# PE's order in the mixer stretches of a two-layer hybrid decoder trunk fixed to the order in which the program emits it

## The chip, the cores and the metric

The kernel runs on one core of one Trainium2 chip. The metric is the device time of one execution in microseconds (us). A core has five engines that run their own instruction streams and wait for one another on semaphores: PE (TensorE, matrix products), DVE (VectorE), ACT (ScalarE), POOL (GpSimd) and SP (SyncE, which here only issues DMAs). PEld in the profile is PE's weight load, which overlaps its matmuls.

## The reference

One step of a trunk with two layers: 256 tokens of a new prompt, and 8 samples of 8 tokens each with 2,048 cached tokens behind them. The kernel keeps both together as T = 320 columns.

```python
def trunk(...):
    for l in range(DEPTH):                     # 2 layers, D_MODEL 1024, D_FF 2816
        x = x + 0.5 * swiglu(rms_norm(x, W['norm_ffn1'][l]), W['ffn1_wi'][l], W['ffn1_wo'][l])
        p = rms_norm(x, W['norm_mix'][l]) @ W['w_in'][l]
        p_hg, p_rw, p_mla = jnp.split(p, [HG_COLS, HG_COLS + RW_COLS], axis=-1)
        o_hg, hg_s = hgrn2_mixer(p_hg, lbs[l], W['hg_norm'][l], hg_s0[l])       # 4 heads of 64
        o_rw, rw_s, rw_sh = rwkv7_mixer(p_rw, rw_sh0[l], rw_s0[l], l, W)        # 4 heads of 64
        q_nope, q_pe, c, k_pe = mla_project(p_mla, pos, l, W)
        o_mla = attend(l, q_nope, q_pe, c, k_pe)      # 8 heads; samples read pages of a cache
        o = jnp.concatenate([o_hg, o_rw, o_mla], axis=-1)
        x = x + o @ W['w_out'][l]
        x = x + 0.5 * swiglu(rms_norm(x, W['norm_ffn2'][l]), W['ffn2_wi'][l], W['ffn2_wo'][l])
    y = rms_norm(x, W['norm_final'])
```

Everything is float32. The outputs are y and the new recurrent states and cache rows.

## The kernel before

x lies transposed, with features on the partitions and the 320 tokens in the columns. Each dense product (the feed-forward parts, the in-projections, w_out) is done with 128x128 weight blocks that are split into a high and a low part in fp32r, by an ACT cast (`split`, L422) and a DVE subtraction (L423); three matmuls of 320 columns make one block (`dense_steps`, `dense_pair`). The weights of the feed-forward parts are streamed on SP's queue, those of the mixers on ACT's, 512 columns at a time.

The program is: first feed-forward part, mixer of layer 0, second and first feed-forward parts, mixer of layer 1, last feed-forward part. In the profiled execution the two mixer stretches lie at about 223 to 613 us and 1051 to 1445 us. A mixer (`mixer`, L550) computes:

- `mla_in` and `mla_q`, the in-projections of the attention, in a plain sequence;
- then two weaves. The first has `rw` (RWKV-7, for each pair of heads `hp` a preparation, a triangular inverse by levels, then `seq` and chunks of 64 tokens), `rw_out`, `sample` (attention over the cached pages: scores into `S`, `exps` at L890, transposes of `S` into `pa` banks, sums with the pages into `pv`) and a `fill` of dense in-projections (`rw_in`, `hg_in`). The second weave has `hg` (HGRN2), `prompt` (the prompt's attention, in `heads`), the rest of `sample`, and `w_out`.

The small sums of `rw` and `hg` are in plain fp32 on 64 partitions each: two heads lie in the two halves of the partitions, `R2 = [slice(0, 64), slice(64, 128)]`, and a loop `for r in R2` emits the matmul of each half. The sums of `sample` have 64 weight columns (96x64 or 128x64). Products into one PSUM bank go by the tags `pd` (2 banks), `pr` (3), `pa` (2) and `pv` (1).

**What sets PE's order.** `weave` (L513) steps the generators. It keeps a planned clock of PE, `self.pe`, which `mm` (L286) and `tr` (L290, transposes) advance; each `yield` names a delay or a due time after which its stream may go on, and the weave takes the first stream that is due. The streams of `rw`, `hg` and `prompt` are urgent: their delays are stretched by `LAG = 2.8`, and what they emit gets a higher priority:

```python
with self.tc.high_priority(offset=1000) if g in self.urgent else ExitStack():
    r = next(g)
f = LAG if g in self.urgent else 1
```

The order that comes out is not the order in which PE runs. The scheduler behind the program (`TileContext(nc, schedule_with_timeline_sim=True)`) takes, on each engine, the ready instruction of the highest priority by its own estimate of the time. So in the mixers a matmul of an urgent stream stands in the middle of another stream's sum as soon as it is thought to be ready, and a dense product is cut into pieces.

The places that the prediction speaks of: the end of `rw_in` and the preparation in `rw` (L1009 to L1056: sigmoid, tanh, sqrt and exp on ACT, a scan, two reciprocals L1039 and products on DVE); `scores`, `soft` and `exps` of `sample` (L871 to L890) with the transposes that follow; `heads` (softmax on DVE L782 to L800 and ACT L796); the ten products into `EX` and `ES` in `hg` (exp at L1330); `mla_in`. In the changed kernel these lines lie 8 to 23 lines further down, `mm` at L294 and `tr` at L298.

Of the kernel before, what the change touches and what calls it, by code (L numbers as in the profile page):

```python
# [19 lines left out]
T = 320  # L20
# [25 lines left out]
FINAL = [(0, 1), (1, 1), (2, 2), (4, 2), (6, 1), (7, 1)]  # L46
FPOOL = (1, 4)
R2 = [slice(0, 64), slice(64, 128)]


KR = 96
# [205 lines left out]
class Kern:  # L257
    def __init__(self, ctx, tc, ap):
        self.ctx, self.tc, self.nc, self.ap = ctx, tc, tc.nc, ap
        P = lambda name, bufs, **k: ctx.enter_context(tc.tile_pool(name=name, bufs=bufs, **k))  # L260
        self.cp = P("cp", 1)
        self.xp = P("xp", 1)
        self.wp = P("wp", 1)
        self.ps = P("ps", 1, space=bass.MemoryType.PSUM)
        self.n = 0
        self.gat, self.early, self.casts = [], [], []
        self.pe = 0.0

        self.st = {"wf": [FBLK, 0, None, None], "wm": [MBLK, 0, self.wp, None]}
        self.cur = "wf"  # L270
# [9 lines left out]
        return self.t(self.ps, [128, 512], tag, bufs=self.BANKS[tag])  # L280


    def mm(self, out, w, x, start, stop):
        m, n = (int(np.prod(a.shape[1:])) for a in (w, x))
        c = max(n, 2 * m) if w.dtype == F32R else 4 * max(n, m)
        self.last = self.nc.tensor.matmul(out, w, x, start=start, stop=stop)  # L286
        self.pe += max(c / 2400 * (0.58 if m <= 64 else 1), 0.032)

    def tr(self, out, x, ident):
        self.nc.tensor.transpose(out, x, ident)  # L290
        self.pe += 0.11 if x.shape[0] > 64 else 0.05

    def tr2(self, out, x, idt):
# [254 lines left out]
            yield from g  # L548

    def mixer(self, l):  # L550
        nc, tc = self.nc, self.tc
        self.l = l
        self.pe, self.ready, self.ended, self.ev = 0.0, {}, [], {}
        xh, xl = self.tiles(self.xh, KD), self.tiles(self.xl, KD)
        pool = lambda name: tc.tile_pool(name=f"{name}{l}", bufs=1)
        with pool("mx") as self.mp, pool("ms") as self.sp, tc.tile_pool(name=f"mk{l}", bufs=1, side="right") as self.tb:
            self.idx_setup(l)
            with pool("mq") as self.ta:
                self.mla_in(xh, xl)
                self.mla_q()  # L560
            sample = self.sample()
            with pool("mr") as self.ta:
                rin = self.rw_in(xh, xl)
                for _ in range(17):
                    next(rin)
                rw = [self.together(*[self.chain(self.rw(hp), self.rw_out(hp)) for hp in range(2)])]
                fill, rws = self.chain(rin, self.hg_in(xh, xl), self.outs()), self.rw_split()
                self.urgent = [*rw, rws]
                self.weave([*rw, *ORDER_A(fill, sample), rws], [*rw, fill, rws])
            with pool("mh") as self.ta, pool("mb") as self.tb:  # L570
                hg, prompt, w_out = [self.together(*[self.hg(hp) for hp in range(2)])], self.prompt(), self.w_out()
                self.urgent = [*hg, prompt]
                order = [*hg, *ORDER_B(prompt, sample), w_out]
                self.weave(order, order)
# [198 lines left out]
    def heads(self, g, kT, V, sums, tag):  # L773
# [35 lines left out]
        nc.vector.tensor_copy(PT[:, 512:768], b1[:, :256])  # L809
        yield 1.5  # L810
        po = self.bank()
        for hh in range(2):
            r = slice(64 * hh, 64 * hh + 64)
            vc = slice((2 * g + hh) * 64, (2 * g + hh) * 64 + 64)
            self.mm(po[r, 0:256], V[:, 0, vc], PT[:, hh * 256:hh * 256 + 256], start=True, stop=False)
            self.mm(po[r, 128:256], V[:, 1, vc], PT[:, 512 + hh * 128:640 + hh * 128], start=False, stop=True)
        self.split(po[:, :TP], self.oh[:, 4 + g, :TP], self.ol[:, 4 + g, :TP])
        yield 0.0

# [194 lines left out]
    def rw(self, hp):  # L1014
# [126 lines left out]
        def seq():  # L1141

            tk = slice(TP, T)
            S0 = self.a([128, 8, 64], f"S0{hp}")
            nc.sync.dma_start(S0.rearrange("p b c -> p (b c)"), self.ap["rws0"][l][:, hp * 512:hp * 512 + 512])
            gmv = self.c("gm")[:, :, None].to_broadcast([128, 8, 64])
            pA = self.bank("pr")[:, :64]
            for r in R2:
                self.mm(pA[r], NK[r, 4, 1, 0, :], nat[r, 4, 2, :], start=True, stop=True)
            R = self.a([128, 64], f"Rs{hp}")  # L1150
            pk = self.bank("pr")
            for r in R2:
                self.mm(pk[r, :], kr[r, 0, tk], S0[r, :, :], start=True, stop=True)
            sel = self.a([128, 8, 64], f"bxb{hp}")
            nc.vector.tensor_tensor(out=sel, in0=pk.rearrange("p (s v) -> p s v", s=8), in1=gmv, op=ALU.mult)
            nc.vector.tensor_reduce(out=R, in_=sel.rearrange("p s v -> p v s"), axis=AX.X, op=ALU.add)
            nc.vector.tensor_tensor(out=R, in0=R, in1=pA, op=ALU.add)
            yield
            M()
            pU = self.bank("pr")[:, :64]  # L1160
            for r in R2:
                self.mm(pU[r], DT[r, 4, :], R[r], start=True, stop=True)
            U = self.a([128, 64], f"Rs{hp}")
            nc.scalar.copy(U, pU)
            vb = self.a([128, 8, 64], f"bk{hp}")
            ub = self.a([128, 8, 64], f"bxb{hp}")
            nc.gpsimd.tensor_tensor(out=vb, in0=nat[:, 4, 2, None, :].to_broadcast([128, 8, 64]), in1=gmv, op=ALU.mult)
            nc.vector.tensor_tensor(out=ub, in0=U[:, None, :].to_broadcast([128, 8, 64]), in1=gmv, op=ALU.mult)
            yield
            M()  # L1170
            pY = self.bank("pr")[:, :64]
            for r in R2:
                self.mm(pY[r], nat[r, 4, 2, :], NK[r, 4, 1, 1, :], start=True, stop=False)
                for s in range(8):
                    ss = slice(s * 8, s * 8 + 8)
                    self.mm(pY[r, ss], S0[r, s, :], kr[r, 1, TP + s * 8:TP + s * 8 + 8], start=False, stop=False)
                self.mm(pY[r], U[r], NK[r, 4, 0, 1, :], start=False, stop=True)
            nc.scalar.copy(Y[:, tk], pY)
            yield
            M()  # L1180
            pS = self.bank("pr")
            for r in R2:
                self.mm(pS[r, :], nat[r, 4, 1, :], vb[r], start=True, stop=False)
                self.mm(pS[r, :], nat[r, 4, 0, :], ub[r], start=False, stop=True)
            nc.gpsimd.tensor_tensor(out=S0, in0=S0, in1=eP[:, 1, TP + 7::8][:, :, None].to_broadcast([128, 8, 64]), op=ALU.mult)
            nc.vector.tensor_tensor(out=S0, in0=S0, in1=pS.rearrange("p (s v) -> p s v", s=8), op=ALU.add)
            nc.sync.dma_start(self.ap["o_rws"][l][:, hp * 512:hp * 512 + 512], S0.rearrange("p s v -> p (s v)"))
            yield
# [3 lines left out]
        for c in range(4):  # L1192
# [2 lines left out]
            pR = self.bank("pr")[:, :64]  # L1195
            for r in R2:
                self.mm(pR[r], NK[r, c, 1, 0, :], nat[r, c, 2, :], start=True, stop=c == 0)
                if c:
                    self.mm(pR[r], kr[r, 0, tk], S[r], start=False, stop=True)
            R = self.a([128, 64], f"R{hp}", 2)  # L1200
            nc.scalar.copy(R, pR)
            next(seq, None)
# [9 lines left out]
            pS = self.bank("pr")[:, :64]  # L1212
            for r in R2:
                self.mm(pS[r], nat[r, c, 1, :], nat[r, c, 2, :], start=True, stop=False)
                self.mm(pS[r], nat[r, c, 0, :], U[r], start=False, stop=True)
            new = self.a([128, 64], f"rst{hp}", 2)
            if c:
# [4 lines left out]
            pY = self.bank("pr")[:, :64]  # L1222
            for r in R2:
                self.mm(pY[r], nat[r, c, 2, :], NK[r, c, 1, 1, :], start=True, stop=False)
                if c:
                    self.mm(pY[r], S[r], kr[r, 1, tk], start=False, stop=False)
                self.mm(pY[r], U[r], NK[r, c, 0, 1, :], start=False, stop=True)
            nc.scalar.copy(Y[:, tk], pY)
            S = new
# [68 lines left out]
    def hg(self, hp):  # L1298
# [97 lines left out]
        M()  # L1396
        pO = self.bank("pr")
        for c in range(4):
            for r in R2:
                o = pO[r, c * 64:c * 64 + 64]  # L1400
                self.mm(o, nat[r, 1, c, :], AT[r, c, :], start=True, stop=c == 0)
                if c:
                    self.mm(o, st[r, c - 1, :], qp[r, c * 64:c * 64 + 64], start=False, stop=True)
        for r in R2:
            o = pO[r, TP:T]
            self.mm(o, nat[r, 1, 4, :], AT[r, 4, :], start=True, stop=False)
            for s in range(8):
                ss = slice(s * 8, s * 8 + 8)
                self.mm(o[:, ss], S0[r, s, :], qp[r, TP + s * 8:TP + s * 8 + 8], start=False, stop=s == 7)
        nc.scalar.copy(O, pO[:, :T])  # L1410
        yield 0.5
        M()
# [104 lines left out]
```

## Time and profile before

| | us |
|---|---|
| median of 3 runs (lowest, highest) | 1680.39 (1679.46, 1684.16) |
| the profiled execution's own time | 1684.91 |
| its span in the profile | 1683.2 |
| PE busy, share of the span | 1640.1, 97% |
| DVE busy, share | 959.5, 57% |
| ACT busy, share | 717.0, 43% |
| mean granted clock of PE | 0.984 |

How to read it: the profile shows one execution. An engine's busy time is that of its own instructions. Matmuls overlap in PE's pipeline, and their ends are modelled, so the time that a matmul takes of PE is read from start to start, not from the duration. A plain fp32 matmul leaves two records in the trace, an fp32r matmul one, so "x24" of a plain fp32 shape is 12 matmuls. Idle time of an engine is put down to what ended it, its releaser.

### The profile page before, as it was taken

To read this page: it belongs to the slowest core of one execution; us is meant where nothing else is said; L and a number is where in the kernel's file an instruction comes from. 1 tells how busy PE (TensorE), PEld (TensorE's weight loads), DVE (VectorE), ACT (ScalarE), POOL (GpSimd) and SP (SyncE) were. 2 spreads that over 40 slices of the span, in tenths; PEclk is the share of its full clock that TensorE was granted. 3 is DMA by queue.
4 is the path that set the end of the run, shared out by engine and by line. 5 is a ranking of instruction groups with operands and counts; after the bars stand their busy time and mean duration, and the time that the engine had idled before them with its cause. 6 is when DMAs were issued, how large, how long until landed. Compare 5 with 4: busy or idle time off the path is not lost. (4 is left out here: it accounts for less than half of the span.)

```text
span 1683.2 us, 33387 instructions
## 1 busy us (share of the span) xinstructions
PE 1640.1 (97%) x13174; PEld 1463.3 (87%) x13174; DVE 959.5 (57%) x1599; ACT 717.0 (43%) x1209; POOL 78.6 (5%) x112
## 2 busy tenths in 40 slices
PE   8999999999999899999999999999999999999998
PEld 8999998777657599999999999987775676999998
DVE  7555447844457475554565554478334665655543
ACT  6444334543253364443354443356142543544432
POOL 0000000200030000000000000002000310000000
PEclk9999999999999899999999999999999998999999
DMA  8555526556663455455555555446366545355552
GB/s 267 150 151 150 151 83 174 178 144 178 190 215 114 137 171 150 149 151 150 150 151 151 150 151 150 111 152 187 108 176 203 176 126 188 108 148 150 150 149 92
DMA packets 130908, 260.05 MB, mean 155 GB/s; under 512 B 17264, under 2 KB 75952, under 8 KB 130624
## 3 DMA queue, kind: packets, MB, share of 16 engines
q1 hardware_dynamic: 111584, 223.58, 44.5%
q10 hardware_dynamic: 19136, 34.28, 6.8%
q8 instruction: 104, 1.70, 0.4%
q0 software_dynamic: 32, 0.07, 0.1%
q14 instruction: 52, 0.43, 0.1%
HBM read 253.39 MB, written 4.47 MB: 153 GB/s over the span
## 5 line engine op out<-in xcount | busy, mean ns | idle before, releaser
L423 DVE TENSOR_TENSOR w<-raw,w 128x1024 fp32r<-128x1024 f32 (+1 forms) x392 | 409.9, 1047 | 317.5 <-ACT w L422 316.0
L422 ACT CAST w<-raw 128x1024 fp32r<-128x1024 f32 (+1 forms) x392 | 355.0, 909 | 441.4 <-PE pd L286 208.4
L286 PE MATMUL pd<-xh,w 128*128 128x320 f32 x1792 | 430.9, 320 | 10.2 <-ACT w L422 8.2
L286 PEld LDWEIGHTS pd<-xh,w 128*128 128x128 f32 x1792 | 310.9, 193 | 25.8 <-ACT w L422 11.6
L286 PE MATMUL pd<-xl,w 128*128 128x320 f32 x896 | 284.4, 319 | 0.0
L286 PE MATMUL pr<-xh,w 128*128 128x320 f32 x1056 | 242.1, 311 | 3.7 <-ACT w L422 2.9
L286 PE MATMUL pa<-xh,w 128*128 128x320 f32 x896 | 201.7, 309 | 0.0
L286 PEld LDWEIGHTS pr<-xh,w 128*128 128x128 f32 x1056 | 178.4, 188 | 6.2 <-ACT w L422 4.2
L286 PEld LDWEIGHTS pd<-xl,w 128*128 128x128 f32 x896 | 172.6, 193 | 7.7 <-issue 6.3
L286 PE MATMUL pr<-xl,w 128*128 128x320 f32 x528 | 162.6, 310 | 0.0
L286 PE MATMUL pd<-hh,w 128*128 128x320 f32 x704 | 158.2, 309 | 0.0
L286 PE MATMUL pr<-hh,w 128*128 128x320 f32 x704 | 158.2, 309 | 0.0
L286 PEld LDWEIGHTS pa<-xh,w 128*128 128x128 f32 x896 | 150.9, 188 | 0.0
L286 PE MATMUL pa<-xl,w 128*128 128x320 f32 x448 | 137.6, 309 | 0.0
L286 PE MATMUL pa<-ct,qlat 96*64 96x256 f32 x768 | 119.5, 390 | 0.2 <-DMA ct<-in_ct 0.2
L286 PEld LDWEIGHTS pd<-hh,w 128*128 128x128 f32 x704 | 118.5, 188 | 0.0
L286 PEld LDWEIGHTS pr<-hh,w 128*128 128x128 f32 x704 | 118.5, 188 | 0.0
L286 PE MATMUL pd<-hl,w 128*128 128x320 f32 x352 | 108.8, 309 | 0.0
L286 PE MATMUL pr<-hl,w 128*128 128x320 f32 x352 | 108.8, 309 | 0.0
L286 PEld LDWEIGHTS pr<-xl,w 128*128 128x128 f32 x528 | 99.2, 188 | 0.4
L470 ACT ACTIVATE fa<-fa 128x320 f32<-128x320 f32 x88 | 41.5, 472 | 134.0 <-DVE fa L469 133.9
L286 PEld LDWEIGHTS pa<-ct,qlat 96*64 96x64 f32 x768 | 58.9, 137 | 37.0 <-issue 14.8
(381 smaller groups left out, 2049.6 us busy)
## 6 DMA issues: line engine op xcount, KB each, us to landing
raw<-in_wf SPq DMA_DIRECT2D x264, 512.0 KB, 3.6
ct<-in_ct SPq DMA_DIRECT2D x256, 144.0 KB, 2.8
raw<-in_wm ACTq DMA_DIRECT2D x128, 256.0 KB, 3.1
cn<-in_cn SPq DMA_DIRECT2D x256, 128.0 KB, 2.4
xT<-in_x SPq DMA_DIRECT2D x4, 320.0 KB, 6.8
wukt<-in_wukt SPq DMA_DIRECT2D x2, 576.0 KB, 5.9
S<-in_rws SPq DMA_DIRECT2D x4, 256.0 KB, 3.4
o_rws<-S SPq DMA_DIRECT2D x4, 256.0 KB, 2.9
```

Of the source, the lines that this page charges most:

```text
L286: self.last = self.nc.tensor.matmul(out, w, x, start=start, stop=stop)
L422: self.cast = nc.scalar.copy(h, src).ins
L423: nc.vector.tensor_tensor(out=lo, in0=src, in1=h.bitcast(F32), op=ALU.subtract)
L470: nc.scalar.activation(a, a, AF.Silu)
```

## The change

`mm` and `tr` pass each PE instruction to a new helper `queued`. While `self.fixed` is set, it makes the instruction depend on the PE instruction emitted before it, without a semaphore (the class `NoSync`), so that the scheduler must keep PE's instructions in the emitted order. `mixer` sets `self.fixed` for its whole length, around the old body, now `mixer_`. The feed-forward parts are not touched. Besides, the sums that ran both (or all) matmuls of one half of the partitions before those of the other now alternate the halves: in `heads` (`po`), in `rw` (`pY`, `pS`, `pR`, in `seq` and in the chunks) and in `hg` (`pO`).

```diff
+NOSYNC = mybir.DependencyInfo(mybir.DependencyClass.NoSync, mybir.DependencyReason.DATA)
...
+        self.fixed, self.last = False, None
...
+    def queued(self, i):
+
+        if self.fixed and self.last is not None:
+            self.tc.add_manual_dep(i.ins, self.last.ins.name, NOSYNC, reason="the order of the trace")
+        self.last = i
+
     def mm(self, out, w, x, start, stop):
...
-        self.last = self.nc.tensor.matmul(out, w, x, start=start, stop=stop)
+        self.queued(self.nc.tensor.matmul(out, w, x, start=start, stop=stop))
...
-        self.nc.tensor.transpose(out, x, ident)
+        self.queued(self.nc.tensor.transpose(out, x, ident))
...
     def mixer(self, l):
+        self.fixed = True
+        self.mixer_(l)
+        self.fixed = False
+
+    def mixer_(self, l):
...
             for r in R2:
                 self.mm(pY[r], nat[r, 4, 2, :], NK[r, 4, 1, 1, :], start=True, stop=False)
-                for s in range(8):
-                    ss = slice(s * 8, s * 8 + 8)
+            for s in range(8):
+                ss = slice(s * 8, s * 8 + 8)
+                for r in R2:
                     self.mm(pY[r, ss], S0[r, s, :], kr[r, 1, TP + s * 8:TP + s * 8 + 8], start=False, stop=False)
+            for r in R2:
                 self.mm(pY[r], U[r], NK[r, 4, 0, 1, :], start=False, stop=True)
...
             for r in R2:
                 self.mm(pR[r], NK[r, c, 1, 0, :], nat[r, c, 2, :], start=True, stop=c == 0)
-                if c:
-                    self.mm(pR[r], kr[r, 0, tk], S[r], start=False, stop=True)
+            for r in R2 if c else ():
+                self.mm(pR[r], kr[r, 0, tk], S[r], start=False, stop=True)
```

The other loops (`po`, both `pS`, the chunks' `pY`, `pO`) are rewritten in the same way.

In numbers, read from the two orders: both kernels have the same 10,651 matmuls and transposes on PE. 4,323 of them stand at another place, all inside the two mixer stretches. The neighbours on PE that use the array in different shapes (128x128, 128x64, 64x64, 64x128) fall from 472 to 288, so 184 fewer switches: 28 fewer from a 64-column sum (128x64) to 64x64, 26 fewer from a 64-column sum to 128x128, and 130 fewer of the other kinds. Of the matmuls of 8 columns (32 in `rw` and 32 in `hg` for each layer), 100 had a neighbour of the same half behind them, and now none has; of the 64x64 ones of 64 columns it falls from 134 to none. The other engines keep their instructions, but for 4 more loads of ACT's function tables (52 to 56), and are ordered anew by the scheduler around the new order of PE.

**The end of `rw_in`, PE, layer 0.** `pr_529` to `pr_531` and `pr_543` to `pr_545` are the preparation's six products of `rw` for the two pairs of heads (`lora` into the sigmoids, `rt` into the norm of the keys), `pd_467` and `pd_522` are in-projections, `pa_...` scores of `sample` with pages `ct`. Before:

```order
L286 MATMUL pa_481_3107<-ct_484_3130,qlat_331_2430 64x256
L286 MATMUL pa_481_3107<-ct_485_3138,qlat_331_2430 64x256
L286 MATMUL pr_529_3369<-lo_442_2910,lora_439_2905 128x320 [waits DMAHW6_49,DVE_49,Activation_49]
L286 MATMUL pr_530_3372<-lo_442_2910,lora_439_2905 128x320
L286 MATMUL pr_531_3375<-rt0_528_3367,cf_1_70 128x320 [waits Activation_49]
L286 MATMUL pd_467_3045<-xh_246_1701,w4_473_3067 128x320 [waits DVE_49]
L286 MATMUL pd_467_3045<-xh_246_1701,w4_472_3066 128x320
L286 MATMUL pd_467_3045<-xl_247_1702,w4_472_3066 128x320
```

Now:

```order
L294 MATMUL pd_522_3352<-xl_247_1702,w4_524_3355 128x320
L294 MATMUL pd_522_3352<-xh_246_1701,w4_525_3356 128x320
L294 MATMUL pr_529_3369<-lo_442_2910,lora_439_2905 128x320
L294 MATMUL pr_530_3372<-lo_442_2910,lora_439_2905 128x320
L294 MATMUL pr_531_3375<-rt0_528_3367,cf_1_70 128x320
L294 MATMUL pr_543_3405<-lo_442_2910,lora_439_2905 128x320 [waits Activation_49]
L294 MATMUL pr_544_3408<-lo_442_2910,lora_439_2905 128x320 [waits Activation_49]
L294 MATMUL pr_545_3411<-rt1_542_3403,cf_1_70 128x320 [waits DVE_49]
L294 MATMUL pa_502_3254<-ct_554_3437,qlat_331_2430 64x256 [waits DMAHW2_49,DMAHW1_49]
```

The first three products stood inside the fourth in-projection of `rw_in`, and now all six stand together behind its seventh and last, inside the first tile of `hg_in`.

**The same stretch on ACT**, from the first sigmoid of `rw` on (`w4` are weight casts, `raw` weight loads, `eP` and `X` exps, `rt` square roots). Before:

```order
L1030 ACTIVATE sw0_526_3365<-pr_529_3369,vec_2_72 128x320 [waits PE_49]
L1033 ACTIVATE rwa0_527_3366<-pr_530_3372,vec_2_72 128x320 [waits PE_49]
L1045 ACT_TABLE_LOAD
L1045 ACTIVATE X0_535_3385<-bxb0_533_3381 128x320 [waits DVE_49]
L1038 ACT_TABLE_LOAD
L1038 ACTIVATE rt0_532_3377<-rt0_532_3377 128x320 [waits DVE_49]
L1046 ACT_TABLE_LOAD
L1046 ACTIVATE eP0_534_3384<-bxb0_533_3381 128x640 [waits Pool_49]
L422 CAST w4_497_3213<-raw_496_3211 128x512 [waits DMAHW6_49,PE_49]
L370 DMA raw_508_3281<-in_wm 128x512 [waits DMAHW0_49,Activation_49]
L1030 ACT_TABLE_LOAD
L1030 ACTIVATE sw1_540_3401<-pr_543_3405,vec_2_72 128x320 [waits PE_49]
```

Now:

```order
L1043 ACTIVATE sw0_526_3365<-pr_529_3369,vec_2_72 128x320 [waits PE_49]
L1046 ACTIVATE rwa0_527_3366<-pr_530_3372,vec_2_72 128x320 [waits PE_49]
L1058 ACT_TABLE_LOAD
L1058 ACTIVATE X0_535_3385<-bxb0_533_3381 128x320 [waits DVE_49]
L1043 ACT_TABLE_LOAD
L1043 ACTIVATE sw1_540_3401<-pr_543_3405,vec_2_72 128x320 [waits PE_49]
L1051 ACT_TABLE_LOAD
L1051 ACTIVATE rt0_532_3377<-rt0_532_3377 128x320 [waits DVE_49]
L1059 ACT_TABLE_LOAD
L1059 ACTIVATE eP0_534_3384<-bxb0_533_3381 128x640 [waits Pool_49]
L1046 ACT_TABLE_LOAD
L1046 ACTIVATE rwa1_541_3402<-pr_544_3408,vec_2_72 128x320 [waits PE_49]
```

Of these twelve rows 4 were table loads before, and 5 are now, since the steps of the two pairs of heads are mixed; from `sw0` to the exp of `S_486` it is 8 before and 9 now.

**The first transposes of the sample's weights, PE, layer 0.** `pa_579` are the transposes of `S_486` after its exp; the products with `kkr`, `bk`, `NK`, `sw` and `X` are those of `rw`'s inverse, `pd_570` is an in-projection of `hg_in`. Before:

```order
L286 MATMUL pr_649_4043<-sw0_622_3883,NK0_620_3881 64x64 [waits DVE_49]
L286 MATMUL pr_649_4043<-sw0_622_3883,NK0_620_3881 64x64 x9
L286 MATMUL pr_651_4056<-kkr0_433_2899,bk0_536_3388 64x128 [waits DVE_49]
L286 MATMUL pr_651_4056<-kkr0_433_2899,bk0_536_3388 64x128 x7
L286 MATMUL pr_653_4067<-sw1_630_3919,NK1_628_3917 64x64 [waits DVE_49]
L286 MATMUL pr_653_4067<-sw1_630_3919,NK1_628_3917 64x64 x9
L290 MATMUL pa_579_3611<-cf_1_70,S_486_3152 128x128 [waits Activation_49]
L286 MATMUL pr_655_4080<-kkr1_436_2902,bk1_550_3424 64x128 [waits Activation_49]
L286 MATMUL pr_655_4080<-kkr1_436_2902,bk1_550_3424 64x128 x7
L290 MATMUL pa_579_3611<-cf_1_70,S_486_3152 128x128 x3
```

Now:

```order
L294 MATMUL pd_570_3559<-xl_247_1702,w4_572_3562 128x320
L294 MATMUL pd_570_3559<-xh_246_1701,w4_573_3563 128x320
L294 MATMUL pd_570_3559<-xh_246_1701,w4_572_3562 128x320
L294 MATMUL pd_570_3559<-xl_247_1702,w4_572_3562 128x320
L294 MATMUL pd_570_3559<-xh_246_1701,w4_573_3563 128x320
L298 MATMUL pa_579_3611<-cf_1_70,S_486_3152 128x128 [waits PE_49,Activation_49]
L298 MATMUL pa_579_3611<-cf_1_70,S_486_3152 128x128 x3
L294 MATMUL pd_570_3559<-xh_246_1701,w4_582_3620 128x320
L294 MATMUL pd_570_3559<-xl_247_1702,w4_582_3620 128x320
```

Before, the products of `rw`'s inverse stood around the transposes, one of them between the first and the other three. Now the in-projection goes on to the transposes without a break, and what stands behind them in program order can't run ahead of them.

## Rows read from the trace of the kernel before

**Rows 1.** The page, part on busy time: engine, us (share) x instructions.

```profile
PE 1640.1 (97%) x13174; PEld 1463.3 (87%) x13174; DVE 959.5 (57%) x1599; ACT 717.0 (43%) x1209; POOL 78.6 (5%) x112
```

**Rows 2.** Windows: length, busy us of PE, PEld, DVE, ACT, POOL, clock, DMA share, GB/s.

```profile
223.00:613.00 390.00, 376.85 (x3596) 289.55 (x3596) 228.41 (x446) 166.70 (x352) 36.11 (x50) 0.98 0.53 159
...
1051.00:1445.00 394.00, 379.29 (x3585) 291.26 (x3584) 226.30 (x443) 164.52 (x349) 36.38 (x50) 0.97 0.52 155
```

**Rows 3.** Waits of PE in 240 to 612 us: us in total, times, longest.

```profile
PE pa L290 <- ACT S L890: 3.7, 2, 1.9
PE pr L286 <- ACT X L1111: 2.6, 1, 2.6
```

**Rows 4.** Timeline of PE at switches: start us, us, operation, tiles, shapes, records.

```profile
328.76 0.31 PE L286 MATMUL pd<-xh,w 128*128 128x320 f32 x1
329.00 2.81 PE L286 MATMUL pa<-ct,qlat 96*64 96x256 f32 x24
331.75 0.42 PE L286 MATMUL pd<-xh,w 128*128 128x320 f32 x1
...
333.56 0.45 PE L286 MATMUL pd<-xh,w 128*128 128x320 f32 x2
333.85 0.31 PE L286 MATMUL pd<-xl,w 128*128 128x320 f32 x1
...
539.56 1.90 PE L286 MATMUL pv<-cn,PT 128*64 128x256 f32 x16
541.29 0.60 PE L286 MATMUL pa<-ct,qlat 96*64 96x256 f32 x2
...
562.65 0.65 PE L286 MATMUL pv<-cn,PT 128*64 128x256 f32 x2
563.23 0.66 PE L290 MATMUL pd<-cf,wuv 128*128 128x128 f32 x4
```

**Rows 5.** Timeline of PE, small sums on halves of the partitions.

```profile
512.35 1.61 PE L286 MATMUL pr<-EX,kE 64*64 64x64 f32 x48
513.90 0.42 PE L286 MATMUL pd<-xl,w 128*128 128x320 f32 x1
...
526.89 0.87 PE L286 MATMUL pr<-lf,S 64*64 64x8 f32 x13
527.57 0.27 PE L286 MATMUL pr<-AT,EX 64*64 64x64 f32 x1
```

**Rows 6.** Timeline of ACT in 300 to 352 us.

```profile
303.35 0.53 ACT L1030 ACTIVATE sw<-pr,vec 128x320 f32<-128x320 f32 x1 [0.91 <-PE pr L286]
...
304.32 1.28 ACT L1045 ACT_TABLE_LOAD   x1
...
309.82 0.60 ACT L422 CAST w<-raw 128x512 fp32r<-128x512 f32 x1
...
342.02 0.73 ACT L890 ACTIVATE S<-S,smx 128x512 f32<-128x512 f32 x1
```

**Rows 7.** Timeline of DVE in the preparation of `rw`.

```profile
326.40 2.15 DVE L1039 RECIPROCAL rt<-rt 128x320 f32<-128x320 f32 x1
```

**Rows 8.** Timeline of PE behind a wait.

```profile
347.79 1.97 PE L286 MATMUL pr<-kkr,bk 64*64 64x128 f32 x16 [2.57 <-ACT X L1111]
```

**Rows 9.** The window that follows (columns of rows 2).

```profile
347.30:350.80 3.50, 3.01 (x21) 2.60 (x21) 1.96 (x4) 0.76 (x3) 0.00 (x0) 0.51 0.07 23
```

**Rows 10.** Timeline of DVE, the softmax of one pair of heads.

```profile
547.81 0.69 DVE L782 TENSOR_TENSOR wuv<-pd,cf 128x512 f32<-128x512 f32 x1 [0.22 <-PE pd L286]
...
557.65 1.01 DVE L800 TENSOR_SCALAR wuv<-wuv,acc 128x256 f32<-128x256 f32 x4
```

**Rows 11.** Timeline of PE, products into `EX`.

```profile
493.48 0.50 PE L286 MATMUL pr<-hgr,lfh 64*128 64x512 f32 x2
...
494.15 0.65 PE L286 MATMUL pa<-ct,qlat 96*64 96x256 f32 x2
```

**Rows 12.** Lines of ACT in 484 to 502 us: busy us, mean ns, idle.

```profile
L1330 ACT ACTIVATE EX<-pr 128x512 f32<-128x512 f32 x8 | 4.6, 603 | 0.3
```

More of the change, by code (lines that the diff above doesn't have):

```diff
@@ L811, in heads @@
         po = self.bank()
[L812 to L816, printed above, removed]
+        vc = lambda hh: slice((2 * g + hh) * 64, (2 * g + hh) * 64 + 64)
+        for hh, r in enumerate(R2):
+            self.mm(po[r, 0:256], V[:, 0, vc(hh)], PT[:, hh * 256:hh * 256 + 256], start=True, stop=False)
+        for hh, r in enumerate(R2):
+            self.mm(po[r, 128:256], V[:, 1, vc(hh)], PT[:, 512 + hh * 128:640 + hh * 128], start=False, stop=True)
         self.split(po[:, :TP], self.oh[:, 4 + g, :TP], self.ol[:, 4 + g, :TP])
@@ L1183, in seq @@
                 self.mm(pS[r, :], nat[r, 4, 1, :], vb[r], start=True, stop=False)
+            for r in R2:
                 self.mm(pS[r, :], nat[r, 4, 0, :], ub[r], start=False, stop=True)
@@ L1214, in rw @@
                 self.mm(pS[r], nat[r, c, 1, :], nat[r, c, 2, :], start=True, stop=False)
+            for r in R2:
                 self.mm(pS[r], nat[r, c, 0, :], U[r], start=False, stop=True)
@@ L1224, in rw @@
                 self.mm(pY[r], nat[r, c, 2, :], NK[r, c, 1, 1, :], start=True, stop=False)
-                if c:
-                    self.mm(pY[r], S[r], kr[r, 1, tk], start=False, stop=False)
+            for r in R2 if c else ():
+                self.mm(pY[r], S[r], kr[r, 1, tk], start=False, stop=False)
+            for r in R2:
                 self.mm(pY[r], U[r], NK[r, c, 0, 1, :], start=False, stop=True)
@@ L1398, in hg @@
         for c in range(4):
+            tk = slice(c * 64, c * 64 + 64)
             for r in R2:
[L1400 to L1403, printed above, removed]
+                self.mm(pO[r, tk], nat[r, 1, c, :], AT[r, c, :], start=True, stop=c == 0)
+            for r in R2 if c else ():
+                self.mm(pO[r, tk], st[r, c - 1, :], qp[r, tk], start=False, stop=True)
         for r in R2:
[L1405 to L1409, printed above, removed]
+            self.mm(pO[r, TP:T], nat[r, 1, 4, :], AT[r, 4, :], start=True, stop=False)
+        for s in range(8):
+            ss = slice(TP + s * 8, TP + s * 8 + 8)
+            for r in R2:
+                self.mm(pO[r, ss], S0[r, s, :], qp[r, ss], start=False, stop=s == 7)
         nc.scalar.copy(O, pO[:, :T])
```

## The prediction

> **What bounds the kernel now.** First the page's busy times: PE is busy for 97% of the span, ACT for 43% [rows 1]. So the time is PE's, and what is worth looking at is where PE waits and what its work costs there. Then the windows of the two stretches that the change touches: in 223 to 613 us PE is busy for 376.9 of 390 us, in 1051 to 1445 us for 379.3 of 394 [rows 2]. That leaves 13.2 and 14.7 us of idle time, and in the feed-forward stretches nothing moves. Third the waits of PE in the first of them: the transposes of `S` wait for its exp (3.7 us in all), and the products of `rw`'s inverse for a copy of `X` (2.6) [rows 3]. The reader is to see that the order before hides nearly everything that ACT and DVE do. What a fixed order can win is therefore in PE's own work, and what it can lose is this cover.
>
> **What the change removes: switches of the array's shape.** 184 neighbours of different shapes go (472 to 288). Prices come from starts in the timeline. In a run, a 64-column sum costs 0.216 us a matmul (8 matmuls from 539.56 to 541.29, 1.73 us), and a dense matmul 0.147 [rows 4]. Going over to the sums of `ct`, the last dense matmul takes 0.24 us (328.76 to 329.00), so the switch costs 0.09. The 12 matmuls behind it take 2.75 us (329.00 to 331.75) against 12 x 0.216 = 2.59, so the way back costs 0.16. A single 64-column matmul between scores and transposes takes 0.58 us (562.65 to 563.23), so leaving such a sum for plain fp32 costs up to 0.36 [rows 4].
>
> - From a 64-column sum to 64x64, 28 fewer: the nearest row is the 0.36; I take 0.31, 8.7 us.
> - From a 64-column sum to 128x128, 26 fewer: some go on to dense (0.16), some to transposes or scores (0.36); I take 0.24, 6.2 us.
> - The other 130: between 0.09 and 0.16, I take 0.14, 18.2 us.
>
> Together 33 us. With every price at its low end (0.09 for the 130, 0.16 for the 54) it is 20 us, with every one at its high end (0.16 and 0.36) 40 us.
>
> **The alternating halves.** 13 records of 8 columns take 0.68 us (526.89 to 527.57), so one matmul (two records) about 0.105 us where its neighbour works in the same half. 48 records of 64 columns in alternating order take 1.55 us (512.35 to 513.90), 0.065 a matmul, with the switches at both ends in it [rows 5]. 100 matmuls of 8 columns had such a neighbour: 100 x 0.04 = 4 us. For the 134 of 64 columns no row parts the two cases; I take 1 us, between 0 and 4. The 48 records write the same bank in both halves, and run at the fast rate.
>
> The Trainium skill speaks against such a gain: "TensorEngine Tiling (Array Packing)", section "Gotcha 1: PSUM Pressure", says that row tiles which differ can't use the same PSUM bank at once. By it the 5 us would be nothing. The 48 records above, with both halves in one bank, contradict it.
>
> So the change takes about 33 + 5 = 38 us from PE's work, 19 in each layer, with ends 20 and 48 us.
>
> **What it adds: waits that lose their cover.** PE can no longer pull a ready product ahead of a waiting one. Four kinds of places, for one layer:
>
> A. *The preparation of `rw`.* Before, the first two sigmoids ran at 303.35 us, and the first exps of the sample's scores at 342.02, 39 us later [rows 6]. In these 39 us PE did in-projections. In the new order the six products of the preparation stand together, and between the third of them and the transposes of `S_486` stand only three products (0.3 us each, as two dense matmuls), 18 matmuls with `ct` (at 0.23, 4.1 us), 30 dense ones (4.4), six small ones (0.5) and some switches (0.7): about 11 us of work. On ACT, from the sigmoid `sw0` to the exp of `S_486`, stand 9 table loads at 1.28 us (11.5), 5 casts and copies at 0.60 (3.0) and 12 activations at about 0.5 (6.0) [rows 6]: 20.5 us. So PE stands still for at least 20.5 - 11 = 9.5 us. On DVE, from the last but two evictions of `rw_in` to the scaled maxima that the exp needs, stand 51 instructions, two of them reciprocals of 2.15 us [rows 7], the others at an estimated 0.46 each, between the 0.25 and 0.69 of [rows 10]: 27 us. If they end last, it is 27 - 11 = 16 us. I take the middle, 12.6, less the 2.6 us that PE waited here before [rows 3, 8]: 10 us, ends 7 and 13.
>
> B. *The heads of `prompt`.* The softmax of one pair of heads is a masked sum and a maximum over 512 columns on DVE (0.69 each), the same over 256 (some 0.4 each), four exps on ACT (some 0.5 each, by the 0.53 of [rows 6]) and four scalings at 557.65 (1.0) [rows 10], with two tiny steps 5.5 us. Before the last pair's transposes PE now has six transposes, 16 small products and one sum of `po`, 3.7 us, so 1.8 us are open. With three similar places (the second score product waits for a bank that DVE frees) I take 5 us, ends 2 and 9.
>
> C. *The products into `EX`.* Ten pairs now stand in a row. One pair takes PE 0.335 us (two pairs from 493.48 to 494.15), an exp of 512 columns 0.60, of which the next one overlaps a little (0.52 I reckon) [rows 11, 12], and three banks lie between. Ten times the difference, with the table load ahead, is 2.5 us; ends 0 and 4.
>
> D. *Small ones.* `mla_in` (weights of the third tile, the sum of squares), pages of `ct` and `cn`, the levels of the inverse, the first block of a w_out tile: I count eight. The longest single waits before took 1.9 and 2.6 us [rows 3]; at 1.5 each that is 12 us, ends 0 and 21.
>
> Together 29.5 us for a layer, 59 for both, ends 18 and 94.
>
> **The clock.** After the idle 2.57 us that end at 347.79 the granted clock is 0.51 for 3.5 us, the lower of its two levels (1.2 of 2.4 GHz) [rows 8, 9]. 3.5 us at half speed cost 1.7 us. One more such window in each layer: 3.5 us, ends 0 and 10.
>
> **The sum.** -38 + 59 + 3.5 = +24.5 us. The profiled execution took 1684.9 us, so it would take 1709; the median of the runs is 4.5 us lower, so I predict **1705 us**. A measurement of this kernel can tell about 0.3% (5 us) from no change.
>
> **The rivals.**
>
> 1. *The cover holds* (faster). The other engines' orders were made anew around PE's, and they have slack: ACT is busy for 43%, DVE for 57%. If they start the preparation early enough that new waits stay under some 16 us a layer, the saved switches win. With half of my waits it is 1680.4 - 38 + 30 = 1672 us, with none 1642. Against it: at A the products that start ACT's chain stand too late, whatever ACT does. Chance 0.25.
> 2. *Both cancel*, new waits of 16 to 21 us a layer: 1675 to 1685 us. Chance 0.12.
> 3. *The waits reach their upper ends* (slower by far): ACT's and DVE's chains alternate step by step, so that A costs 13 us, B 9, C 4 and the small ones 19 a layer: 1680.4 - 38 + 2 x 45 + 5 = 1737 us. Chance 0.08.
> 4. *The halves gain nothing*, which is the rule on PSUM banks as a mechanism of this kernel: two neighbours that write both halves of one bank still take 0.105 each. That adds 5 us to the sum, 1710 us; the 48 records speak against it. Chance 0.02, within the forecast's range.
>
> That the scheduler might have run the mixers in the emitted order anyway is excluded: 4,323 matmuls stand elsewhere.
>
> **How the numbers follow.** The forecast, new waits of 21 to 45 us a layer, 1685.5 to 1735 us, has 0.55 with the fourth rival in it. Slower by over 0.3% is 0.55 + 0.08 = 0.63, the same 0.12, faster 0.25. The range must reach into the first rival: down to 1660 it leaves out about 0.10, and up to 1735 another 0.08.
>
> **What would show it.** Right: PE's busy time in the two stretches falls, by some 38 us in sum, and its idle time in each grows from 13 to 15 us to over 35; the longest wait is PE's for `S` from the exp, near 350 us and again some 828 us later; a wait for `EX`' banks and for DVE in `heads` appears. Wrong: idle time in the stretches of under 30 us each would make the waits too large in the sum, and a fall of PE's work of less than 25 us in all the switches. If the idle time at A is there but stands elsewhere than at the transposes of `S`, its place is wrong and its size may be right.

## The result and the profile after

The changed kernel takes 1727.43 us (median of 4 runs, 1724.24 to 1728.23), the kernel before in the same comparison 1682.28 us (4 runs, 1679.46 to 1686.05). The ratio is 1.0265, with a 95% interval of 1.0245 to 1.0284: slower by 45 us. The forecast was 1705 us, slower by 24.5, in a range from 1660 to 1735.

First the page of the changed kernel: busy times (as in [rows 1]) and the granted clock of PE in 40 slices, in tenths.

```profile
PE 1614.5 (94%) x13174; PEld 1459.3 (85%) x13174; DVE 956.6 (55%) x1599; ACT 724.2 (42%) x1213; POOL 79.3 (5%) x112
...
PEclk9999998989989999999999999998999898999999
```

PE is busy for 25.6 us less than in [rows 1], and yet the span grew from 1683.2 to 1726.3 us. So PE's idle time grew by 43.1 + 25.6 = 68.7 us. The next view is the mean granted clock of the core, which was 0.984 before:

```profile
core 0: 1726.3 us, clock 0.968
```

The clock has two levels, and the windows show 0.50 or 0.51 where it is at the lower one. There are 9 such stretches before and 18 now. The last lines of the two views that list them all, before first, give their length in sum and how much of it PE was busy:

```profile
sum 52.30, PE 43.12 PEld 35.11 DVE 19.76 ACT 16.77 POOL 2.15; mean PE 4.79 PEld 3.90 DVE 2.20 ACT 1.86 POOL 0.24
sum 110.40, PE 82.31 PEld 62.77 DVE 66.10 ACT 47.20 POOL 27.42; mean PE 4.57 PEld 3.49 DVE 3.67 ACT 2.62 POOL 1.52
```

So PE works for 39 us more at the lower level than before.

The windows of the two stretches and of the feed-forward between them show where (columns of [rows 2]).

```profile
223.00:636.00 413.00, 367.85 (x3592) 290.61 (x3591) 226.78 (x446) 168.92 (x353) 36.87 (x50) 0.93 0.52 151
636.00:1074.00 438.00, 438.00 (x2985) 437.68 (x2984) 247.65 (x339) 187.98 (x244) 0.00 (x0) 1.00 0.51 150
1074.00:1490.00 416.00, 364.95 (x3603) 288.74 (x3602) 225.59 (x443) 170.06 (x352) 36.31 (x50) 0.94 0.49 147
```

The feed-forward stretch takes 438 us, and the same stretch of before took 438 too (613 to 1051 us). All the loss lies in the mixers: 390 us became 413, 394 became 416. PE's idle time there rose from 13.2 and 14.7 us [rows 2] to 45.2 and 51.0, the mean clock fell from 0.98 and 0.97 to 0.93 and 0.94.

Then PE's waits in the first layer (us in total, times, longest), which answer to [rows 3]:

```profile
PE pa L298 <- ACT S L903: 9.1, 1, 9.1
PE pd L294 <- DVE qa L678: 5.4, 1, 5.4
PE pa L294 <- DMA ct<-in_ct: 5.4, 5, 1.6
...
PE pa L294 <- ACT S L884: 2.3, 1, 2.3
...
PE pr L294 <- ACT EX L1348: 1.5, 1, 1.5
PE pd L298 <- DVE wuk L813: 1.4, 1, 1.4
PE pr L294 <- ACT X L1124: 1.3, 1, 1.3
PE pd L294 <- ACT pPT L821: 1.2, 2, 0.6
...
PE pd L298 <- DVE wuv L795: 0.7, 1, 0.7
```

and in the second:

```profile
PE pa L298 <- ACT S L903: 11.0, 1, 11.0
PE pa L294 <- DMA ct<-in_ct: 8.1, 9, 2.0
PE pd L294 <- DVE qa L678: 6.0, 1, 6.0
PE pa L294 <- ACT S L884: 3.9, 1, 3.9
```

Two places stand out: the transposes of the sample's `S` (place A of the prediction), and a wait for `qa` in the projections. `qa` is DVE's eviction of the first projection tile, and the fifth tile needs its bank. At A the timelines of PE, ACT and DVE, one after the other, tell what ended last.

```profile
346.37 0.70 PE L294 MATMUL pa<-cT,qlat 96*64 96x64 f32 x8 [2.31 <-ACT S L884]
...
347.92 0.73 PE L294 MATMUL pd<-xh,w 128*128 128x320 f32 x2
348.45 0.47 PE L294 MATMUL pd<-xl,w 128*128 128x320 f32 x1
...
351.92 0.47 PE L294 MATMUL pd<-xh,w 128*128 128x320 f32 x1
361.43 1.12 PE L298 MATMUL pa<-cf,S 128*128 128x128 f32 x4 [9.05 <-ACT S L903]
```

```profile
333.20 0.53 ACT L1043 ACTIVATE sw<-pr,vec 128x320 f32<-128x320 f32 x1 [1.14 <-PE pr L294]
...
355.07 1.28 ACT L903 ACT_TABLE_LOAD   x1
360.56 0.72 ACT L903 ACTIVATE S<-S,smx 128x512 f32<-128x512 f32 x1 [4.21 <-DVE smx L899]
```

```profile
333.76 0.82 DVE L1054 TENSOR_TENSOR_SCAN bxb<-cf,sw 128x320 f32<-128x320 f32 x1 [0.36 <-ACT sw L1043]
...
348.13 2.15 DVE L1052 RECIPROCAL rt<-rt 128x320 f32<-128x320 f32 x1 [1.10 <-ACT rt L1051]
...
360.39 0.14 DVE L899 TENSOR_SCALAR smx<-smx 128x1 f32<-128x1 f32 x1
```

ACT had its table loaded at 356.4 us and then stood still for 4.2 us: what PE waits for in the end is DVE, which had gone through the preparation of `rw` and the sample's maxima from 333.76 to 360.5 us, 26.7 us. It was not busy throughout (length, busy us and instructions of DVE, clock, DMA share, GB/s):

```profile
333.76:360.50 26.74, 20.22 (x34) 0.73 0.51 147
```

For the other 6.5 us it waited for ACT, longest for the copy of `S` (2.0) and the second `sw` (1.9). And around each such wait of PE the clock is at its lower level (windows around the waits for `qa`, for `S` from L884 and for `S` from L903; columns of [rows 2]):

```profile
264.00:270.80 6.80, 4.63 (x17) 4.66 (x18) 4.34 (x8) 2.31 (x6) 0.00 (x0) 0.50 0.24 77
345.90:352.80 6.90, 6.01 (x30) 5.49 (x30) 5.35 (x9) 4.31 (x8) 0.86 (x1) 0.51 0.69 203
356.20:366.40 10.20, 4.97 (x20) 4.45 (x22) 6.53 (x12) 5.96 (x11) 4.17 (x5) 0.50 0.05 19
```

In these 23.9 us PE worked for 15.6. A dense matmul takes 0.265 us there from start to start (two from 347.92 to 348.45), where the prediction read 0.147 at the upper level. So of PE's time at the lower level 45% is lost by this reading, 50% by the ratio of the two levels.

### The profile page after: what moved, and what is told of

The parts are those of the page before. It is cut to its first block, busy times and chain, and to the rows that moved or that the text cites. A ratio compares the mean times of both kernels' runs of the same rounds, so it can differ in the third digit from the quotient of the medians.

```text
span 1726.3 us, 33388 instructions
## 1 busy us (share of the span) xinstructions
PE 1614.5 (94%) x13174; PEld 1459.3 (85%) x13174; DVE 956.6 (55%) x1599; ACT 724.2 (42%) x1213; POOL 79.3 (5%) x112
## 4 chain that ended last, share of the span: by engine, by line
PE 83%; ACT 5%; DMA 5%; DVE 4%; issue 2%; SPq 2%; ACTq 0%; DVEq 0%
PE pd L294 32%; PE pr L294 29%; PE pa L294 17%; PE pv L294 3%; DMA ct<-in_ct 2%; DMA raw<-in_wm 2%; PE pa L298 1%; ACT S L903 1%; SPq L874 1%; SPq L917 0%; DMA raw<-in_wf 0%; DVE w L431 0%; PE pd L298 0%; SPq L858 0%; DMA xT<-in_x 0%
## 5 line engine op out<-in xcount | busy, mean ns | idle before, releaser
L294 PEld LDWEIGHTS pd<-xh,w 128*128 128x128 f32 x1792 | 315.9, 195 | 36.7 <-issue 19.1
L294 PE MATMUL pa<-ct,qlat 96*64 96x256 f32 x768 | 106.2, 400 | 13.7 <-DMA ct<-in_ct 13.5
```

Of the source, the lines that this page charges most:

```text
L294: self.queued(self.nc.tensor.matmul(out, w, x, start=start, stop=stop))
```

## The experiments

Edits are against the changed kernel. Idle time is PE's, as the sum of its waits in the two stretches (before 27.1 us, changed kernel 95.5).

### The two halves of the change apart: e1_halves_only, e2_order_only

```diff
     def mixer(self, l):
-        self.fixed = True
         self.mixer_(l)
-        self.fixed = False
```

> The halves alternate in the sums as in the change, PE's order is left to the scheduler as before. Theory (the loss comes from waits that lose their cover under the fixed order): 1677 to 1688 us, within 0.4% of before, idle time of PE in the two mixer stretches 12 to 17 us each. Rival 1 (the alternation itself slows the sums, since both halves write one bank): over 1700 us.

Measured: 1677.78 us (median of 10 runs) against 1685.88, ratio 0.9956 [0.9938, 0.9973]. Idle 31.6 us, clock 0.987, PE busy 1629.1 us. PE's timeline shows the sums that now alternate:

```profile
529.35 1.05 PE L294 MATMUL pr<-lf,S 64*64 64x8 f32 x32
530.26 0.25 PE L294 MATMUL pr<-AT,EX 64*64 64x64 f32 x1
```

32 records (16 matmuls) take 0.91 us, 0.057 a matmul, where the 13 records of [rows 5] took 0.68 us: 0.105, or 0.085 if three records to a run of 16 are missing. Both halves write one bank here. Met: the halves are worth 0.44%, some 7 us, and they are no part of the loss.

The second kernel has the order fixed and the old loops (those behind the minus signs in the diff of the change).

> PE's order is fixed as in the change, the loops over the halves are those of before. Theory: slower than the change by what the 8-column sums lose next to their own half, 2 to 8 us, so 1729 to 1736 us. Rival 1 (the alternation is what costs): under 1700 us.

Measured: 1738.95 us, 1.0327 [1.0285, 1.0369]; idle 95.4 us, clock 0.964. That is 3 us over the expected 1729 to 1736: under a fixed order the halves are worth some 10 us (ratios 1.0327 and 1.0265). The loss is the order's.

### Where in the mixer: e3_fixed_projections, e4_fixed_first_weave, e8_fixed_second_weave

The order is fixed for one part of the mixer only: in the attention's projections, in the first weave, in the second. For e3:

```diff
             sample = self.sample()
+            self.fixed = False
```

> The order is fixed only in the projections of the attention ahead of the weaves; halves as in the change. In the trace of the change this part lasts 13.8 us longer in layer 0 (to 286.7 us instead of 272.9). Theory of several places: 1682 + 2 x 13 = 1708 us (1702 to 1714). Rival 2 (the wait for the exps in the first weave is the loss, the projections only shift work): 1680 to 1690 us.

Measured: 1724.21 us, 1.0234 [1.0187, 1.0281]; idle 60.6 us, clock 0.974. Missed by 10 us. Its waits in the first layer:

```profile
PE pv L294 <- DMA cn<-in_cn: 5.6, 8, 1.2
PE pd L294 <- DVE qa L679: 4.8, 1, 4.8
PE pa L298 <- ACT S L904: 3.6, 3, 2.4
PE pr L294 <- ACT X L1125: 3.2, 1, 3.2
```

Of these only the wait for `qa` lies in the part that was fixed. `qh`, which the projections make for the attention, is first read at 280.6 us, against 268.5 before: 12 us of the loss in this layer lie in the projections. The rest lies in the weaves, which were not fixed: behind projections that end later, the scheduler laid them out anew, and worse.

For e4 and e8 the two assignments stand around one weave each; in e4 the first steps of `rw_in`, which stand ahead of it, are fixed too.

> The order is fixed only in the first weave; halves as in the change. About 110 of the 184 switches go (work 15 to 19 us less in each layer), the wait for the exps of the first scores stays (9 to 11 us in each layer) with other waits of about 8. Theory of several places: 1684 us (1674 to 1694). Rival 2 (this place is the loss): over 1705 us.

Measured: 1706.48 us, 1.0141 [1.0102, 1.018]; idle 70.4 us, clock 0.977. Waits in the first layer:

```profile
PE pa L298 <- ACT S L903: 9.1, 1, 9.1
PE pa L294 <- DMA ct<-in_ct: 7.6, 7, 2.2
```

The number is the rival's, its reason isn't borne out: the wait for `S` is as long as in the whole change, but it is a quarter of the idle time in a layer (9.1 of 35.2 us). Many short waits make up the rest.

> The order is fixed only in the second weave; halves as in the change. By subtraction of the parts (change +45 us, projections +8 to 11 us in each layer within the change, first weave alone +20): 1682 + 7, so 1680 to 1700 us. If the parts do not add up, because the scheduler lays out the free parts anew around a fixed one: over 1705 us.

Measured: 1715.28 us, 1.017 [1.0126, 1.0214]; idle 62.7 us, clock 0.976. This too is over what subtraction gave (1680 to 1700). The single parts cost 38, 21 and 31 us (e3, e4, e8), 90 together, and the whole change 45. **The parts don't add up**, since what isn't fixed is laid out anew each time. So no share of the 45 us can be read from a part that is fixed alone; the next runs keep the order fixed throughout and mend one place each.

### The two long waits mended: e5_close_early, e6_prep_free, e7_both

In e5 the norm's sum, which starts the chain of DVE that `qa` ends, is emitted ahead of the third tile's products:

```diff
         first.append(self.bank("pr")[:, :T])
+        self.norm_close()
         self.dense(first[2], KD, xh, xl)
-        self.norm_close()
```

> The change, with the norm's last sum emitted ahead of the third tile of the projections instead of behind it. One dense tile is 24 x 0.147 = 3.5 us. Theory of several places: PE's wait for qa in the projections (5.4 and 6.0 us in the change) falls by about 3.5 us in each layer, and a half clock window behind it goes: 1727 - 7 to 14, so 1713 to 1720 us. Rival 3 (a wait that is taken away comes back at the next place): 1723 us or more.

Measured: 1717.09 us, 1.0196 [1.0164, 1.0228]; idle 85.2 us. Met. The wait for `qa` is gone from the list, and the tile's first reader starts (last but one column: first and last start)

```profile
L294 PE MATMUL pd<-qh,w x36: 304/308/417, 270.8 to 1126.5; 128*128 128x320 f32 x36
```

at 270.8 us, where it was 279.8 in the changed kernel: 9.0 us earlier, of which 5.4 are the wait. The others are a second wait behind it, which is shorter now, and the stretch at the lower clock; how they share is not shown.

In e6 the six products of the preparation of `rw` are left out of the chain, so that the scheduler may put them earlier:

```diff
     def queued(self, i):
+        if self.free:
+            return
...
         M()
+        self.free = True
...
         self.mm(ps, self.c("bd1"), sq, start=True, stop=True)
+        self.free = False
```

> The change, with the six first products of rw's preparation outside the fixed order, so that they can run as early as before. Theory: PE's wait for S from its exp (9.1 and 11.0 us) falls to about 3 us in each layer, with less time at the half clock: 1727 - 13 to 25, so 1702 to 1714 us. Rival 3: 1720 us or more, since the wait only moves to the products of rw's inverse or to the next transposes.

Measured: 1717.46 us, 1.02 [1.0171, 1.0229]; idle 83.5 us, clock 0.970. Missed by 3 us. The wait at A did fall as expected (first layer; 3.3 in the second):

```profile
PE pa L296 <- DMA ct<-in_ct: 6.6, 6, 2.0
...
PE pa L300 <- ACT S L905: 3.4, 1, 3.4
```

From 9.1 and 11.0 us it fell by 13.4 in both layers together, and idle time by 12.0, so hardly any of it came back at the next wait: those for pages of `ct`, 6.6 and 7.7 us, were 5.4 and 8.1 in the changed kernel. What did not come is the expected gain in the clock, 0.970 against 0.968, and PE is busy for 2 us more (1616.7). Why the clock stayed low is open.

> The edits of the last two runs together. Theory of separate places: the two gains add up, 1727 - 20 to 39, so 1688 to 1707 us, still slower than before, since some ten smaller waits stay. Rival 3: over 1712 us.

Measured with both edits: 1696.48 us (5 runs), 1.0071 [1.0046, 1.0097]; idle 69.9 us, clock 0.975. Met. Together the two edits give 31 us by the medians, more than the 10 + 10 that each gives alone. In the profiled executions it is 26 us of span (1700.0) for 12 and 10, and 25.6 us of idle time for 10.3 and 12.0: the gains add up and a little more, and where the surplus comes from is not shown. Both are shown to be places of the loss, and they are some two thirds of it.

### Is the wait real idle time: e9_filler

44 dense matmuls, whose results are overwritten, stand right ahead of the first transposes of `S` in each layer; the planned clock is not advanced by them.

```diff
+            if p == 0 and ch == 0:
+                pe = self.pe
+                for i in range(44):
+                    self.mm(po[:, :T], self.xh[:, i % KD, 0:128], self.xh[:, i % KD, :], start=True, stop=True)
+                self.pe = pe
```

> The change, with 44 more dense matmuls (6.5 us at full clock) in each layer, into a bank that is still free, right ahead of the transposes that wait for S; their results are overwritten. Everything else of the order in the weaves is as in the change. Theory (PE stands still there for 9.1 and 11.0 us, and the idle time lowers the clock behind it): the added work lies in the wait, and with PE busy less of the half clock follows, so 1720 to 1728 us, no slower than the change's 1727 and perhaps some us faster, with a wait for S of 2 to 5 us. Rival 4 (PE has no real idle time there): 1727 + 13 = 1740 us.

Measured: 1741.01 us, 1.0336 [1.0319, 1.0354], 13.6 us more than the changed kernel; idle 92.9 us. Missed by 13 us: by its total this is the number of the case in which work there isn't covered. PE's timeline says otherwise for the place itself:

```profile
351.18 6.62 PE L294 MATMUL pv<-xh 128*128 128x320 f32 x44
361.49 1.11 PE L298 MATMUL pa<-cf,S 128*128 128x128 f32 x4 [3.70 <-ACT S L903]
```

The added work of 6.6 us is absorbed: the transposes start at 361.49 us, where they started at 361.43. The loss comes later in this layer: the last sum of the mixer starts at 650.00 us, where it started at 636.48, while in the second layer, with the same filler, only 1 us more is lost (1503.19 against 1488.72). The windows from the transposes to that last sum, first of the changed kernel, then of this run (columns of [rows 2]), split the loss:

```profile
361.40:636.50 275.10, 251.89 (x2859) 187.94 (x2860) 143.45 (x299) 107.03 (x252) 23.54 (x27) 0.95 0.52 156
361.50:650.00 288.50, 258.31 (x2858) 192.54 (x2859) 143.80 (x299) 108.79 (x252) 23.51 (x27) 0.92 0.50 149
```

With the same work PE is busy for 6.4 us more, at a lower mean clock, and idle for 7.0 us more. So the wait at A is idle time that work can fill, and the total of this run tells nothing on it. What brings the later waits is open.

### The spacing: e10_lag_17, e11_projections_close_early, e12_free_lag_17

`LAG` stretches the delays of the urgent streams in the planned order. A free scheduler may still put whatever product it thinks ready into a stretch that is too long; with a fixed order the stretch is what PE does.

```diff
-LAG = 2.8
+LAG = 1.7
```

> The version with both mended places, with LAG 1.7 instead of 2.8. Theory: LAG stretches the planned delays of the urgent streams for a scheduler that still pulls ready products ahead; with the order fixed it sets the true distances, and 2.8 is the wrong one: waits of PE in the mixers fall from 70 us by 10 to 20, so 1672 to 1688 us, as fast as before or a little faster. Rival 5 (what is left are waits that no spacing of the streams moves): 1691 us or more.

Measured, on top of e7's two edits: 1662.78 us (5 runs, 1660.87 to 1666.57) against 1683.31, ratio **0.9883 [0.9865, 0.9901]**. This beats both kernels, by 9 us more than the expected range. Its page, and its windows up to the last sum of each mixer:

```profile
PE 1590.5 (96%) x13174; PEld 1442.2 (87%) x13174; DVE 954.2 (57%) x1599; ACT 718.1 (43%) x1207; POOL 83.2 (5%) x112
```

```profile
223.00:603.50 380.50, 350.89 (x3594) 278.46 (x3593) 226.05 (x446) 165.17 (x350) 38.57 (x50) 0.99 0.57 163
...
1042.00:1423.10 381.10, 357.85 (x3594) 283.84 (x3593) 224.18 (x443) 164.16 (x347) 38.54 (x50) 0.96 0.54 160
```

The mixers are some 9 and 13 us shorter than in [rows 2]. The clock is 0.986 over the span, close to that of before (0.984), and PE is busy for 49.6 us less than in [rows 1]. This reads what a fixed order takes from PE's work almost without the clock: 0.002 x 1683 = 3 us of it are the clock, some 46 us the order and the halves. It is not quite the order of the change, as the spacing is another. Idle time is still 51.2 us in the two stretches, nearly twice that of before.

> LAG 1.7 without the fixed order: the halves alternate, the scheduler orders PE as before. A control of the fast version. Theory (the shorter delays help because the order is fixed, and the 20 us under before come from the switches that the fixed order saves): no faster than the halves alone, 1678 us or more. Rival 6 (LAG 1.7 is better in any case, and the fixed order adds nothing): 1655 to 1668 us.

The control, the free order with the halves and the same `LAG`: 1735.1 us (6 runs), 1.0318 [1.0289, 1.0346]; idle 66.6 us, clock 0.983. Met: the spacing alone is no gain. Its longest wait in each layer:

```profile
PE pa L298 <- ACT S L901: 4.1, 1, 4.1
...
PE pd L298 <- DVE wuk L811: 4.8, 1, 4.8
```

The idle time is 40 us over that of before, and yet the clock is nearly the same (0.983 and 0.984): idle time in sum does not set it. Of the two values tried, 2.8 suits the free order (1677.8 against 1735.1), 1.7 the fixed one (1696.5 against 1662.8, both with e7's edits). A free order with e5's early sum was not run; in the kernel before, PE has no wait for `qa`, so little is to be expected of it.

> The order fixed only in the projections, with the early norm sum. In the run with the projections alone 20 us of the 38 were lost inside the projections, the rest in the weaves, which the scheduler laid out anew. Theory: the projections lose only 2 to 4 us now, and the weaves their 18 as before: 1697 to 1710 us. If the loss in the weaves comes from the late projections: 1682 to 1692 us.

Measured, as e3 with e5's edit: 1694.19 us, 1.007 [1.0051, 1.009]; idle 39.0 us, clock 0.987. It falls between the two expectations, slightly nearer the second: 27 of the 38 us of e3 go with one sum that is emitted earlier (38 and 11 us over the kernel before, each in its own comparison). `qh` is first read at 269.8 us, 1.3 us later than before, where it was 12.1 in e3: with the second layer alike, some 21 of the 27 us lie in the projections themselves. How much of the loss in the free weaves came with the late projections is therefore not settled. Why 11 us remain is open.

## Why the prediction was right in direction and short in size

**The sum.** Forecast −38 + 59 + 3.5. Measured in the spans, idle time is +68.7, and PE's busy time, −25.6, holds both the work and the clock. The sums of the stretches at the lower level part the two: PE was busy in them for 43.1 us before and for 82.3 now, and of that 45 to 50% is lost, 19 to 22 us before and 37 to 41 now. So the clock is some +18 (up to 20), and PE's work some −44. Sum +43.

**The step that failed is the clock.** The prediction put one more window of 3.5 us in each layer, 3.5 us in all with an end at 10. It had seen a window of 3.5 us behind a wait of 2.57 [rows 8, 9], and forecast some 30 us of new waits a layer beside it, but priced one window. The row was right, its count was wrong: there are 9 more such stretches, 58 us in sum, and behind the longer waits they last 6.8 and 10.2 us. This is some 15 of the 18.5 us by which the forecast fell short; the waits add 10, and the larger gain in work takes 6 back. That these offset one another in part is luck.

**The gain in PE's work** was forecast at 38 us, ends 20 and 48, and is some 44 (46 in e10). By its own test ("PE's busy time in the two stretches falls, by some 38 us in sum") the forecast would seem too large: it fell by 376.85 + 379.29 − 367.85 − 364.95 = 23.3 us, under the 25 named as a sign of error. That test was badly built, as busy time has the clock in it. The halves, forecast at 5 us, are worth about 6: e1's busy time fell by 11.0 us, 5 of them with its clock (0.003 x 1680). No run parts the kinds of switches, so their single prices stay estimates. The rule of the Trainium skill that was weighed there ("TensorEngine Tiling (Array Packing)", section "Gotcha 1: PSUM Pressure": row tiles that differ can't use the same bank at once) did not keep the halves from gaining: e1 takes 0.057 us a matmul with both in one bank. Whether two of them are in the bank at one moment no row shows.

**Place A** was right in place and size, and its size owes something to luck. Forecast 10 us a layer over before; PE waits 2.3 + 9.1 and 3.9 + 11.0 us, which less the 2.6 of before is 8.8 and 12.3. It stands at the transposes of `S`, at 352.4 us and again 848 us later (828 forecast). The prediction took the middle between ACT's end (9.5) and DVE's (16). The rows show DVE last, in 26.7 us for the 27 reckoned, but not as reckoned: it did 34 instructions in 20.2 us, not 51 in 27, and the other 6.5 us are waits for ACT. So the two chains alternate, and neither end alone gives the time. What keeps the wait from 16 us is PE, which from 333.8 to 352.4 us is busy for 15.8 rather than 11:

```profile
333.80:352.40 18.60, 15.79 (x85) 11.13 (x84) 12.08 (x19) 15.85 (x21) 3.85 (x5) 0.73 0.54 150
```

The mean clock of 0.73 puts half of this stretch at the lower level; at the upper one the 11 us would be about right. The step on the clock made the wait shorter here, and PE's work longer.

**B** was about right, **C** too large: of the waits in `heads` the whole list has 4.0 us in the first layer (1.4 for `wuk`, 1.2 for `pPT`, 0.7 for `wuv`, and 0.7 in three smaller ones) where 5 were forecast, for `EX` 1.5 and, in the second layer, 0.9 where 2.5 a layer. **D** was too small: what is left of the first layer's 32 us is 32 − 8.8 − 4.0 − 1.5 = 18 us, for which 12 were forecast (ends 0 and 21). The second longest wait of all, 5.4 and 6.0 us for `qa`, was in D as one of eight at 1.5. The prediction had named `mla_in` and its sum of squares, but did not follow the chain from the norm's sum over ACT and DVE to the eviction that frees the fifth tile's bank, as it did for A.

**The rivals.** That the cover holds (1642 to 1672) is refuted for this kernel: idle time rose by 68.7 us. What spoke for it, ACT at 43% and DVE at 57% busy, is true and didn't help at A and at `qa`, since these chains are started by PE's own late products; e5 and e6 show it by starting them earlier. With those and another spacing e10 comes to 1662.8 us, inside that rival's numbers. The rival of the upper ends (1737) is nearest in total, but not by its reasons: B and C stayed under their upper ends, and the clock took their place.

## What to carry to other kernels

Where an engine's order is fixed, the planned distances decide: start the products that begin long chains on other engines first, and set the spacing anew for the fixed order (here 1.7 for 2.8, 34 us), as a spacing that was tuned under a free scheduler need not suit it, nor the other way round. Price a new long wait on PE with the stretch at the lower clock around it: here 69 us more of idle time went with some 18 us of PE's work lost besides. A fix of one part alone isn't a share of the whole, since the scheduler lays out the rest anew: keep all else fixed, and mend one place.

## What the runs showed of the hardware that was not expected

Not expected was that a single wait of 2.3 us in a stretch that is otherwise busy stands in 6.9 us at the lower clock, nearly as much as one of 5.4 us (6.8), and that 69 us more of idle time went with 58 us more at that level, while e12's 40 us more in the two stretches went with some 6 (mean clock 0.983 over 1732 us). The other surprise is the rate of the alternating halves: 0.057 us for a matmul of 8 columns, against 0.085 to 0.105 in the same half, though both halves write one bank of PSUM.
